# The MLP's first two groups and the fourth of seven products: one more group in seven products, and a weight sum made in SBUF

## The chip, the cores and the metric

The kernel runs on one core of one Trainium2 chip. The metric is the device time of one execution in microseconds (us). A core has five engines with instruction queues of their own: TensorE (PE; its weight loads, PEld, are shown apart), VectorE (DVE), ScalarE (ACT), GpSimd (POOL) and SyncE (SP). They wait for each other through semaphores. SP and POOL issue the transfers of this kernel (DMA); the names SPq and POOLq stand for their queues. An engine works through its instructions in the order in which the program lists them, so an instruction that waits holds up everything behind it.

## The reference

One layer of a hybrid encoder on 512 tokens of width 1024, in float32: an input projection, forgetting attention and a gated linear recurrence side by side, cross-attention to 256 memory tokens, and an MLP.

```
h = h + concat(fox_out, rec) @ w_out
h = h + memory_cross_attention(rmsnorm(h), mem_n, w_xq, w_xkv, w_xo)
u = rmsnorm(h, norm_ff_g) @ w1          # w1: 1024 x 4096
h = h + square(relu(u)) @ w2            # w2: 4096 x 1024
return rmsnorm(h, final_norm_g)
```

This case is about the last three lines.

## The kernel before

**Float32 in three products.** TensorE multiplies in a format of fewer bits (fp32r). So each float32 operand is split into a high part and a low part, and a product is made as hi·hi + hi·lo + lo·hi. A weight block arrives raw from DRAM (`wr…`, issued by SP); ScalarE copies it to its high part (`wh…`, line L181 in `split_of`) and VectorE subtracts that from the raw data for the low part (`wl…`, L185). Both parts have four buffers, so a split can start when the product four places earlier has ended. `unit()` keeps splits up to four units ahead of the products and loads up to eight units ahead (`LOADS`).

**Groups.** The MLP's 4096 hidden columns are worked off in 8 groups of 512. For a group, the *up* set computes u = x2 · W1 for its 512 columns, ScalarE applies relu and square, and the *down* set adds the square times the group's rows of W2 to the residual `acc`. The order is up 0, up 1, down 0, up 2, down 1, and so on to up 7, then down 6 and 7 together.

**Seven products.** An up or a down set may be made like a Strassen-Winograd product: weights and data are each cut into 2 x 2 blocks, and seven products of sums of blocks take the place of eight products of blocks. Before, up sets 2 to 7 (`SEVEN`) and all down sets are made so; up sets 0 and 1 are made in full, from "panels" (`next_panel`, `mlp_up`), in four quarters of 24 matmuls of 512 columns. The weight operands of the seven products, by name, with Wrc the block in row r, column c: "1" is W00, "2" is W10, "3" is W11, "5" is W00 + W01, "7" is W01 + W11, "6" is W11 + "5", "4" is W10 + "6". The products are worked off as 1, 5, 6, 2, 7, 3, 4 (`PRODUCTS`).

**Weight sums.** The four sums of a set (`SUMS`) are made in DRAM, long ahead. SP copies the first block from DRAM to a DRAM tile `wsu…` (up) or `wsd…` (down); POOL then issues an accumulating DMA that adds the second block or sum (`Presum.emit`, L444); and SP loads the result into SBUF like any weight block. In the names that follow, `wsd65` is the sum for product 5 of down set 6. `COPIES` says with which weight panel how many of the copies go out. `PACE` sets the POOL accumulates: from a given amount of TensorE work on, one goes out every so many microseconds of TensorE work, and each is given a wait for the matmul at which its time came.

**An up set of seven products** (`mlp_up7`) uses three banks of PSUM. Product 1 goes to bank U. ScalarE copies U to bank V (`uV<-uU`, L1406), and product 2 is added there. Product 5 goes to bank Y, and ScalarE copies it out to `y5` (L1409). Product 6 is added to U, so it stands behind the copy to V. Then ScalarE copies U to bank Y (`uY<-uU`, L1411), where product 3 is added; product 7 is added to U, so it stands behind that copy. VectorE reads U + y5 into SBUF before product 4 is added to U. A product is 24 matmuls of 256 columns.

**The data's sums.** `x_sums` makes the sums of blocks of x2 that products 5, 6, 3 and 7 need: per sum two or three VectorE instructions (`xs_d`), a ScalarE copy to the high part (`xs_hi`) and a VectorE subtraction (`xs_lo`). In the code before it is stepped in group 1. In group 0, after two of its four quarters, the code squares the residual and adds it up (`sj<-acc`, L1666), makes e2 from that on POOL, and scales the residual by e2 (`acc<-acc,e`, L1673).

**What sets the order.** The code is written in one order, and a scheduler of the framework lists the instructions of each engine, by their dependences and priorities; the splits are written with a lower priority (`ahead(PW)`). So the listed order can differ from the code's.

Of the kernel before, what the change touches and what calls it, by code (L numbers as in the profile page):

```python
# [13 lines left out]
ALU = mybir.AluOpType  # L14
# [3 lines left out]
S = 512  # L18
# [4 lines left out]
WT = 256  # L23
# [3 lines left out]
HG = 512  # L27
# [9 lines left out]
FX = (4.4, 4.4, 5.4, 5.4), (3.3, 3.9, 4.5, 5.1)  # L37
X1, X2, X3, X4 = 1.5, 2.0, 1.5, 2.0
NEG = -3.0e38
SEVEN = (2, 3, 4, 5, 6, 7)  # L40
RAWS, HB, LOADS = 6, 4, 8
COPIES = {7: 2, 16: 1, 17: 0, 21: 1, 29: 2}
PACE = (183.0, 4.6), (306.0, 6.0), (385.0, 9.0)


@with_exitstack
def emit(
# [49 lines left out]
    def s4(shape, name, dt=F32):  # L97
        return s4p.tile([P] + shape, dt, tag="s4", name=name)
# [45 lines left out]
    specs = []  # L144
# [16 lines left out]
        for j in range(4):  # L161
            specs.append(panel(w, j * WT))
    NG = DFF // HG
    for g in range(2):
        for j in range(2):
            specs.append(panel(w1, g * HG + j * WT))
    stream = []
    state = {"used": 0, "halves": 0}
    copies, copied = deque(), set()
    UW, UK = WT + FH, KC // 2  # L170
# [7 lines left out]
    def split_of(hi, lo, raw):  # L178
        def split(what="hl"):
            if "h" in what:  # L180
                ac.activation(hi, raw, AF.Copy)  # L181
            if "v" in what:
                ve.tensor_copy(hi, raw)
            if "l" in what:
                ve.tensor_tensor(lo, raw, f(hi), ALU.subtract)  # L185

        return split

    def load_unit(name, spec, ks, parts=1, between=None):
# [12 lines left out]
        for q in range(parts):  # L202
# [208 lines left out]
    hn_hi, hn_lo = act_tile("hn_hi"), act_tile("hn_lo")  # L411
    xTd = drp.tile([4, P, 2, S], F32, name="xTd")

    SUMS = {"5": ("00", "01"), "7": ("01", "11"), "6": ("11", "5"), "4": ("10", "6")}

    def block1(g, rc):
        r, c = int(rc[0]), int(rc[1])
        n0 = g * HG + c * WT
        return w1[r * S : (r + 1) * S, n0 : n0 + WT].rearrange("(k p) n -> p k n", p=P)

    def block2(g, rc):
        r, c = int(rc[0]), int(rc[1])
        k0 = g * HG + r * 2 * P
        return w2[k0 : k0 + 2 * P, c * S : (c + 1) * S].rearrange("(k p) n -> p k n", p=P)

    wsum = {}

    def sum_jobs(kind, g):
        block, shape = (block1, [P, UK, WT]) if kind == "u" else (block2, [P, 2, S])
        for name in SUMS:  # L430
            wsum[kind, g, name] = drp.tile(shape, F32, name=f"ws{kind}{g}{name}")

        def first(name):
            dma = nc.sync.dma_start(wsum[kind, g, name], block(g, SUMS[name][0]))
            copied.add((kind, g, name))
            return dma

        def sums():
            for name, (_, b) in SUMS.items():
                while (kind, g, name) not in copied:  # L440
                    copies.popleft()()
                src = wsum[kind, g, b] if b in SUMS else block(g, b)
                more = {"max_dma_last_dim": 2048} if b in SUMS else {}
                yield gp.dma_start(wsum[kind, g, name], src, accum_op=ALU.add, **more)  # L444

        return [lambda name=name: first(name) for name in SUMS], sums()

    class Presum:
        def __init__(self):
            self.jobs, self.spent, self.next, self.at = deque(), 0.0, PACE[0][0], None  # L450

# [23 lines left out]
    presum = Presum()  # L475
    sets = []
    for g in range(DFF // HG):
        sets.append(sum_jobs("d", g))
        if g + 2 in SEVEN:
            sets.append(sum_jobs("u", g + 2))  # L480
    for i in range(0, len(sets), 2):
        for some in zip(*(c for c, _ in sets[i : i + 2])):
            copies.extend(some)
# [168 lines left out]
    for hp in range(2):  # L652
        wt = next_panel()
# [265 lines left out]
    for c in range(NT):  # L919
# [162 lines left out]
    for n in range(len(pairs) + 2):  # L1082
        if n < len(pairs):
            p, tb = pairs[n]
# [97 lines left out]
    _, wo_rest = residual(mx_hi, mx_lo, g_x, x1_hi, x1_lo, "wo", ssq1, (4, 5, 6, 7, 0, 1, 2, 3), 1)  # L1182
# [119 lines left out]
    for i in range(2):  # L1302
        gp.dma_start(gfin[i], final_norm_g[i * S : (i + 1) * S].partition_broadcast(P))
    HS = S // 2
    units, unit_q = {}, deque()
    sqs, comb, hbs = {}, {}, {}
    PRODUCTS = ("1", "5", "6", "2", "7", "3", "4")
    QUAD = {"1": "00", "2": "10", "3": "11"}
    raw_n = [0]

    def raw_tile(name):
        raw_n[0] += 1
        if raw_n[0] % RAWS == 4:
            return t4(f"wr{name}")
        if raw_n[0] % RAWS in (0, 2):
            return wrp.tile([P, D], F32, tag="wr", name=f"wr{name}", padded_shape=[P, UK * UW])
        return s4([D], f"wr{name}")

    load_q = deque()

    def add_unit(key, shape, src):

        name = "".join(map(str, key))
        box = []

        def load():
            raw = raw_tile(name).rearrange("p (k n) -> p k n", k=shape[0])
            nc.sync.dma_start(raw, src())
            box.append(raw)

        def prep():
            while not box:
                load_q.popleft()()
            unit = new_parts(shape, name)
            with ahead(PW):
                split_of(unit[0], unit[1], box[0])()
            units[key] = unit

        unit_q.append((key, prep))
        load_q.append(load)  # L1340

    def up_units(g):
        if g in SEVEN:
            for name in PRODUCTS:
                add_unit(("u", g, name), [UK, WT], lambda name=name: block1(g, QUAD[name]) if name in QUAD else wsum["u", g, name])
            return
        for j in range(2):
            for n in range(2):
                add_unit(("u", g, j, n), [UK, WT], lambda j=j, n=n: block1(g, f"{n}{j}"))

    def down_units(gs):
        for name in PRODUCTS:
            for g in gs:
                add_unit(("d", g, name), [2, S], lambda g=g, name=name: block2(g, QUAD[name]) if name in QUAD else wsum["d", g, name])

    def unit(*key):

        while key not in units:
            unit_q.popleft()[1]()
        got = units[key]  # L1360
        at = order.index(key)
        while unit_q and len(order) - len(unit_q) < at + 4:
            unit_q.popleft()[1]()
        while load_q and len(order) - len(load_q) < at + LOADS:
            load_q.popleft()()
        return got
# [266 lines left out]
        dma_a(tb, o)  # L1633
        scale_b(tb, half, o, r, gfin[half])

    for g in range(NG):
        if g >= 2:
            up_units(g)
        if 1 <= g < NG - 1:
            down_units((g - 1,))  # L1640
    down_units((NG - 2, NG - 1))
    order = [k for k, _ in unit_q]
# [2 lines left out]
    def mlp_up_group(g):  # L1645
        if g in SEVEN:
            yield from mlp_up7(g)
            return
        for j in range(2):
            if g < 2:  # L1650
                wt = next_panel()
                if (g, j) == (1, 1):
                    for _ in range(2):
                        unit_q.popleft()[1]()
            else:
                wt = tuple(list(x) for x in zip(*(unit("u", g, j, n) for n in range(2))))
            yield from mlp_up(g, j, wt)

    ups = mlp_up_group(0)
    next(ups)  # L1660
    to_tok(KC - 2)
    to_tok(KC - 1)
    next(ups)
    ms2 = sm(NT, "ms2")
    for tb in range(NT):
        ac.activation(k4([D], f"sj{tb}"), acc[tb], AF.Square, scale=1.0 / 32.0, accum_out=ms2[:, tb : tb + 1])  # L1666
# [4 lines left out]
    gp.tensor_scalar(eps3, eps3, EPS, 0.0, op0=ALU.mult, op1=ALU.add)  # L1671
    for tb in range(NT):
        ac.activation(acc[tb], acc[tb], AF.Copy, scale=e2[:, tb : tb + 1])  # L1673
    for _ in ups:
        pass
    hidden_sums(0)
    sums = x_sums()
    for g in range(1, NG):
        for n, _ in enumerate(mlp_up_group(g)):
            hidden_ahead((g - 1, PRODUCTS[0]), min(n, HB))  # L1680
            if g == 1:
                next(sums, None)
                next(sums, None)
        hidden_sums(g)
        if g < NG - 1:
            for _ in mlp_down((g - 1,)):
                pass
# [34 lines left out]
```

## Time and profile before

| | |
|---|---|
| median of 3 runs | 756.41 us (756.36 to 757.88) |
| profiled execution | 756.48 us, span 754.5 us |
| TensorE busy | 746.1 us, 99% of the span |
| VectorE, ScalarE, POOL busy | 537.4, 431.1, 190.3 us |
| DMA traffic | 162.85 MB, mean 216 GB/s |
| group 0, up 0 and up 1 in full | 430.06 to 474.50 us |
| down 0 | 474.50 to 493.54 us |
| up 3 | 532.76 to 552.91 us |

The span is the stretch of the profiled execution between its first and last instruction; the execution's own time is a little longer. An engine's busy share is an average over the whole; which engine ends last in a stage is read from windows over that stage and from the waits. A row of the timeline gives start, duration, engine, line, operation, output<-inputs, and in brackets how long the engine was idle before it and who ended that. Instructions of one engine overlap a little, so the time from start to start is what one costs in a row.

### The profile page before, as it was taken

To read this page: it belongs to the slowest core of one execution; us is meant where nothing else is said; L and a number is where in the kernel's file an instruction comes from. 1 tells how busy PE (TensorE), PEld (TensorE's weight loads), DVE (VectorE), ACT (ScalarE), POOL (GpSimd) and SP (SyncE) were. 2 spreads that over 40 slices of the span, in tenths; PEclk is the share of its full clock that TensorE was granted. 3 is DMA by queue.
4 is the path that set the end of the run, shared out by engine and by line. 5 is a ranking of instruction groups with operands and counts; after the bars stand their busy time and mean duration, and the time that the engine had idled before them with its cause. 6 is when DMAs were issued, how large, how long until landed. Compare 5 with 4: busy or idle time off the path is not lost.

```text
span 754.5 us, 12053 instructions
## 1 busy us (share of the span) xinstructions
PE 746.1 (99%) x4501; PEld 648.9 (86%) x4501; DVE 537.4 (71%) x844; ACT 431.1 (57%) x715; POOL 190.3 (25%) x274
## 2 busy tenths in 40 slices
PE   9999999999999999999999999999999999999996
PEld 6889888888888988888888888898989899999985
DVE  5647873677878756745546558978787887879697
ACT  5655555655756532334434396657575757574873
POOL 7207531333342237620121211111000111000014
PEclk9999999999999999999999999999999999999999
DMA  8641987567947899996668879898979797977332
GB/s 251 196 117 57 310 262 226 177 225 252 312 165 222 264 280 290 287 245 128 140 151 182 179 127 312 198 314 229 296 186 298 190 281 205 265 220 248 121 112 112
DMA packets 112444, 162.85 MB, mean 216 GB/s; under 512 B 6482, under 2 KB 73595, under 8 KB 112387
## 3 DMA queue, kind: packets, MB, share of 16 engines
q1 hardware_dynamic: 91186, 123.80, 49.9%
q0 software_dynamic: 20608, 37.25, 27.2%
q10 hardware_dynamic: 592, 1.05, 0.4%
q8 instruction: 35, 0.57, 0.3%
q14 instruction: 23, 0.18, 0.1%
HBM read 157.87 MB, written 62.93 MB: 293 GB/s over the span
## 4 chain that ended last, share of the span: by engine, by line
PE 95%; DVE 1%; ACT 1%; POOL 1%; issue 1%; ACTq 0%; POOLq 0%
PE U L1528 4%; PE U L1527 4%; PE U L1529 4%; PE uU L1402 3%; PE uU L1401 3%; PE uU L1400 3%; PE xq L253 2%; PE wo L253 2%; PE xq L254 2%; PE xw L253 2%; PE xq L255 2%; PE xw L255 2%; PE u L255 2%; PE xw L254 2%; PE wo L255 2%; PE u L254 2%
## 5 line engine op out<-in xcount | busy, mean ns | idle before, releaser
L185 DVE TENSOR_TENSOR wld<-wrd,whd 128x1024 fp32r<-128x1024 f32 x56 | 69.6, 1244 | 17.4 <-ACT whd L181 17.3
L181 ACT ACTIVATE whd<-wrd 128x1024 fp32r<-128x1024 f32 x56 | 59.2, 1057 | 24.6 <-PE uV L1401 8.0
L181 ACT ACTIVATE whu<-wru 128x1024 fp32r<-128x1024 f32 x42 | 44.5, 1059 | 44.9 <-PE uU L1401 18.2
L185 DVE TENSOR_TENSOR wlu<-wru,whu 128x1024 fp32r<-128x1024 f32 x42 | 50.4, 1223 | 14.5 <-ACT whu L181 14.4
L1527 PE MATMUL U<-whd,hb 128*128 128x512 f32 x120 | 46.8, 390 | 0.0
L1528 PE MATMUL U<-wld,hb 128*128 128x512 f32 x120 | 46.8, 390 | 0.0
L1529 PE MATMUL U<-whd,hb 128*128 128x512 f32 x120 | 46.7, 389 | 0.0
L444 POOL DMA_DIRECT2D wsd<-in_w_dram x16 | 16.8, 1050 | 91.5 <-PE U L1529 27.9
L444 POOL DMA_DIRECT2D wsd<-wsd x16 | 14.3, 894 | 98.4 <-PE uU L1402 18.0
L1012 POOL TENSOR_SCALAR bi<-nF,Ft 128x128 f32<-128x128 f32 (+3 forms) x32 | 20.7, 656 | 60.2 <-PE pt L1044 34.7
L444 POOL DMA_DIRECT2D wsu<-in_w_dram x12 | 14.1, 1176 | 58.8 <-PE xq L255 11.4
L1155 ACT ACTIVATE x_hi<-hT,gv 128x512 fp32r<-128x512 f32 x16 | 11.5, 717 | 27.7 <-DVE hT L1154 27.7
L1402 PE MATMUL uU<-x_hi,wlu 128*128 128x256 f32 x96 | 27.2, 283 | 0.0
L1400 PE MATMUL uY<-xs_hi,whu 128*128 128x256 f32 x96 | 27.2, 283 | 0.0
L1401 PE MATMUL uY<-xs_lo,whu 128*128 128x256 f32 x96 | 27.2, 283 | 0.0
L1402 PE MATMUL uY<-xs_hi,wlu 128*128 128x256 f32 x96 | 27.2, 283 | 0.0
L1400 PE MATMUL uU<-xs_hi,whu 128*128 128x256 f32 x96 | 27.2, 283 | 0.0
L1401 PE MATMUL uU<-xs_lo,whu 128*128 128x256 f32 x96 | 27.2, 283 | 0.0
L1402 PE MATMUL uU<-xs_hi,wlu 128*128 128x256 f32 x96 | 27.2, 283 | 0.0
L1401 PE MATMUL uU<-x_lo,whu 128*128 128x256 f32 x96 | 27.2, 283 | 0.0
L1400 PE MATMUL uU<-x_hi,whu 128*128 128x256 f32 x96 | 27.1, 283 | 0.0
L1529 PEld LDWEIGHTS U<-whd,hb 128*128 128x128 f32 x120 | 22.5, 188 | 4.7
(995 smaller groups left out, 2655.2 us busy)
## 6 DMA issues: line engine op xcount, KB each, us to landing
wsd<-in_w_dram SPq DMA_DIRECT2D x32, 512.0 KB, 5.7
wrd<-wsd SPq DMA_DIRECT2D x32, 512.0 KB, 6.3
wsu<-in_w_dram SPq DMA_DIRECT2D x24, 512.0 KB, 7.1
wrd<-in_w_dram SPq DMA_DIRECT2D x24, 512.0 KB, 6.2
wru<-wsu SPq DMA_DIRECT2D x24, 512.0 KB, 6.2
wru<-in_w_dram SPq DMA_DIRECT2D x18, 512.0 KB, 5.8
wsd<-in_w_dram POOLq DMA_DIRECT2D x16, 512.0 KB, 8.0
wsd<-wsd POOLq DMA_DIRECT2D x16, 512.0 KB, 6.8
```

The lines of the kernel that those rows point to most:

```text
L181: ac.activation(hi, raw, AF.Copy)
L185: ve.tensor_tensor(lo, raw, f(hi), ALU.subtract)
L253: te.matmul(ps, wh, hi, start=n_ == 0 and not begun, stop=False)
L254: te.matmul(ps, wh, lo, start=False, stop=False)
L255: at = te.matmul(ps, wl, hi, start=False, stop=k == order[-1])
L444: yield gp.dma_start(wsum[kind, g, name], src, accum_op=ALU.add, **more)
L1400: te.matmul(ps[:, i, :], whi[:, k, ws], xh[:, k, :], start=begin, stop=False, skip_group_check=True)
L1401: te.matmul(ps[:, i, :], whi[:, k, ws], xl[:, k, :], start=False, stop=False, skip_group_check=True)
L1402: at = te.matmul(ps[:, i, :], wlo[:, k, ws], xh[:, k, :], start=False, stop=k == UK - 1, skip_group_check=True)
L1527: te.matmul(ps, hi, whi[:, k, :], start=begin, stop=False, skip_group_check=True)
L1528: te.matmul(ps, hi, wlo[:, k, :], start=False, stop=False, skip_group_check=True)
L1529: at = te.matmul(ps, lo, whi[:, k, :], start=False, stop=k == 1, skip_group_check=True)
```

## The change

Two things are changed in the MLP, with the tables that go with them.

1. Group 1's up set is made of seven products as well. Only group 0 still uses panels. `x_sums` is stepped during group 0's last two quarters, and the squares and the scaling of the residual are written behind group 0's loop. (Their lines are L1676 and L1683 then.)
2. The sum for product 4 is no longer made in DRAM. When product 6's raw tile has been split, POOL adds W10 from DRAM onto the raw tile in SBUF (L1349), and product 4's unit is split from that same tile. This holds for up and down sets, 15 in all. It has no load of its own. Product 6's raw tile is kept in `raws` for it; the rotation of the other raw buffers goes from 6 to 5.

```diff
-SEVEN = (2, 3, 4, 5, 6, 7)
-RAWS, HB, LOADS = 6, 4, 8
-COPIES = {7: 2, 16: 1, 17: 0, 21: 1, 29: 2}
-PACE = (183.0, 4.6), (306.0, 6.0), (385.0, 9.0)
+SEVEN = (1, 2, 3, 4, 5, 6, 7)
+RAWS, HB, LOADS = 5, 4, 8
+COPIES = {7: 2, 16: 1, 17: 0, 21: 1}
+PACE = (183.0, 4.7), (306.0, 11.5)
...
-    SUMS = {"5": ("00", "01"), "7": ("01", "11"), "6": ("11", "5"), "4": ("10", "6")}
+    SUMS = {"5": ("00", "01"), "7": ("01", "11"), "6": ("11", "5")}
...
     for g in range(DFF // HG):
+        if g + 1 in SEVEN:
+            sets.append(sum_jobs("u", g + 1))
         sets.append(sum_jobs("d", g))
-        if g + 2 in SEVEN:
-            sets.append(sum_jobs("u", g + 2))
...
-        if raw_n[0] % RAWS == 4:
+        if raw_n[0] % RAWS == 3:
             return t4(f"wr{name}")
...
         def load():
-            raw = raw_tile(name).rearrange("p (k n) -> p k n", k=shape[0])
-            nc.sync.dma_start(raw, src())
+            if part == "4":
+                box.append(raws.pop((kind, g)))
+                return
+            if part == "6":
+                raw = raws[kind, g] = s4(shape, f"wr{name}")
+            else:
+                raw = raw_tile(name).rearrange("p (k n) -> p k n", k=shape[0])
+            if part in SUMS:
+                src = wsum[kind, g, part]
+            else:
+                src = block(g, QUAD[part])
+            nc.sync.dma_start(raw, src)
             box.append(raw)
 
         def prep():
             while not box:
                 load_q.popleft()()
             unit = new_parts(shape, name)
             with ahead(PW):
                 split_of(unit[0], unit[1], box[0])()
+            if part == "6":
+                gp.dma_start(box[0], block(g, "10"), accum_op=ALU.add)
             units[key] = unit
...
-    for g in range(NG):
-        if g >= 2:
-            up_units(g)
-        if 1 <= g < NG - 1:
+    for g in range(1, NG):
+        up_units(g)
+        if g < NG - 1:
             down_units((g - 1,))
...
     next(ups)
+    sums = x_sums()
+    next(sums)
+    next(sums)
+    for _ in ups:
+        next(sums)
+        next(sums)
     ms2 = sm(NT, "ms2")
...
-    for _ in ups:
-        pass
     hidden_sums(0)
-    sums = x_sums()
     for g in range(1, NG):
         for n, _ in enumerate(mlp_up_group(g)):
             hidden_ahead((g - 1, PRODUCTS[0]), min(n, HB))
             if g == 1:
-                next(sums, None)
                 next(sums, None)
```

How the listed order changes is shown at three places. On ScalarE, from group 0's second quarter on, before (`u001` is the bank of group 0's second quarter, `u010` of its third, `sq00` a hidden tile):

```order
L1666 ACTIVATE sj0_4683,ms2_4682<-acc0_4336 128x1024
L1666 ACTIVATE sj1_4685,ms2_4682<-acc1_4337 128x1024
L1666 ACTIVATE sj2_4687,ms2_4682<-acc2_4338 128x1024
L1666 ACTIVATE sj3_4689,ms2_4682<-acc3_4339 128x1024
L1369 ACTIVATE sq00_4633<-u001_4654 128x512
L1673 ACTIVATE acc0_4336<-acc0_4336,e2_4691 128x1024
L1370 ACTIVATE sq00_4633<-sq00_4633 128x512
L1673 ACTIVATE acc1_4337<-acc1_4337,e2_4691 128x1024
L1673 ACTIVATE acc2_4338<-acc2_4338,e2_4691 128x1024
L1673 ACTIVATE acc3_4339<-acc3_4339,e2_4691 128x1024
L181 ACTIVATE wh36a_4700<-wr36a_4702 128x1024
L1369 ACTIVATE sq01_4738<-u010_4712 128x512
```

After, from the third quarter on, first part (`xs_hi` is a sum of x2):

```order
L1377 ACTIVATE sq01_4705<-u010_4679 128x512
L1676 ACTIVATE sj0_4744,ms2_4743<-acc0_4313 128x1024
L1378 ACTIVATE sq01_4705<-sq01_4705 128x512
L1457 ACTIVATE xs_hi_4659<-xs_d_4661 128x1024
L1676 ACTIVATE sj1_4746,ms2_4743<-acc1_4314 128x1024
L1676 ACTIVATE sj2_4748,ms2_4743<-acc2_4315 128x1024
L1676 ACTIVATE sj3_4750,ms2_4743<-acc3_4316 128x1024
L1377 ACTIVATE sq01_4705<-u011_4712 128x512
```

and directly behind these rows:

```order
L1683 ACTIVATE acc0_4313<-acc0_4313,e2_4752 128x1024
L1378 ACTIVATE sq01_4705<-sq01_4705 128x512
L1683 ACTIVATE acc1_4314<-acc1_4314,e2_4752 128x1024
L1683 ACTIVATE acc2_4315<-acc2_4315,e2_4752 128x1024
L1683 ACTIVATE acc3_4316<-acc3_4316,e2_4752 128x1024
L180 ACTIVATE whu16_4774<-wru16_4772 128x1024
L180 ACTIVATE whu12_4781<-wru12_4779 128x1024
L1414 ACTIVATE uV1_4815<-uU1_4771 128x512
```

The squares and the scalings have moved from around the second quarter's relu to the third's and the fourth's; behind them come the splits of up 1's products 6 and 2 and its copy of bank U to V.

On ScalarE in up set 2, before (`whu24` is the high part for product 4):

```order
L181 ACTIVATE whu27_5173<-wru27_5070 128x1024
L1406 ACTIVATE uV2_5170<-uU2_5138 128x512
L1476 ACTIVATE hb12_5302<-sq11_4898 128x512
L181 ACTIVATE whu23_5205<-wru23_5093 128x1024
L1409 ACTIVATE y52_5203<-uY2_5172 128x512
L181 ACTIVATE whu24_5236<-wru24_5117 128x1024
L1411 ACTIVATE uY2_5172<-uU2_5138 128x512
```

and after:

```order
L180 ACTIVATE whu27_5237<-wru27_5136 128x1024
L1414 ACTIVATE uV2_5234<-uU2_5203 128x512
L180 ACTIVATE whu23_5270<-wru23_5160 128x1024
L1417 ACTIVATE y52_5268<-uY2_5236 128x512
L1484 ACTIVATE hb12_5366<-sq11_4770 128x512
L180 ACTIVATE whu24_5301<-wru26_5090 128x1024
L1419 ACTIVATE uY2_5236<-uU2_5203 128x512
```

The split for product 4 stands in its place as before, ahead of the copy of U to bank Y, and now reads `wru26`, the raw tile of product 6.

On POOL around up sets 4 and 5, after (L443 is an accumulate into DRAM, L1349 one into SBUF; `wru46` is the raw tile of product 6 of up 4):

```order
L443 DMA wsd65_232<-in_w2_dram 256x1x512
L443 DMA wsu77_230<-in_w1_dram 512x1x256
L1349 DMA wru46_5900<-in_w1_dram 128x4x256
L443 DMA wsd67_233<-in_w2_dram 256x1x512
L1349 DMA wrd36_6084<-in_w2_dram 128x2x512
L443 DMA wsu76_231<-wsu75_229 256x512
L443 DMA wsd66_234<-wsd65_232 256x512
L1349 DMA wru56_6305<-in_w1_dram 128x4x256
```

Before, this queue held accumulates into DRAM alone, as here for the sums of sets 4 to 6:

```order
L444 DMA wsu56_223<-wsu55_221 256x512
L444 DMA wsd34_220<-wsd36_219 256x512
L444 DMA wsu54_224<-wsu56_223 256x512
L444 DMA wsd45_225<-in_w2_dram 256x1x512
L444 DMA wsu65_229<-in_w1_dram 512x1x256
```

So the accumulates into SBUF stand between those into DRAM, which wait for their place in TensorE's work.

More of the change, by code (lines that the diff above doesn't have):

```diff
@@ L163, in emit @@
     NG = DFF // HG
-    for g in range(2):
-        for j in range(2):
-            specs.append(panel(w1, g * HG + j * WT))
+    for j in range(2):
+        specs.append(panel(w1, j * WT))
     stream = []
@@ L1304, in emit @@
     HS = S // 2
-    units, unit_q = {}, deque()
+    units, raws, unit_q = {}, {}, deque()
     sqs, comb, hbs = {}, {}, {}
@@ L1319, in emit, with add_unit @@
     load_q = deque()
-    def add_unit(key, shape, src):
+    def add_unit(key, shape):
+        kind, g, part = key[:3]
         name = "".join(map(str, key))
+        block = block1 if kind == "u" else block2
         box = []
         def load():
-            raw = raw_tile(name).rearrange("p (k n) -> p k n", k=shape[0])
-            nc.sync.dma_start(raw, src())
+            if part == "4":
[10 more added lines that the diff above has]
+            nc.sync.dma_start(raw, src)
             box.append(raw)
@@ L1342, in up_units @@
     def up_units(g):
[L1343 to L1349, printed above, removed]
+        for part in PRODUCTS:
+            add_unit(("u", g, part), [UK, WT])
     def down_units(gs):
@@ L1353, in down_units @@
             for g in gs:
-                add_unit(("d", g, name), [2, S], lambda g=g, name=name: block2(g, QUAD[name]) if name in QUAD else wsum["d", g, name])
+                add_unit(("d", g, name), [2, S])
     def unit(*key):
@@ L1649, in mlp_up_group @@
         for j in range(2):
[L1650 to L1656, printed above, removed]
+            wt = next_panel()
+            if j == 1:
+                for _ in range(2):
+                    unit_q.popleft()[1]()
             yield from mlp_up(g, j, wt)
```

## The prediction

> **What bounds the kernel now.** I read the page first: span, busy shares, clock, chain.
>
> ```profile
> span 754.5 us, 12053 instructions
> PE 746.1 (99%) x4501; PEld 648.9 (86%) x4501; DVE 537.4 (71%) x844; ACT 431.1 (57%) x715; POOL 190.3 (25%) x274
> PEclk9999999999999999999999999999999999999999
> PE 95%; DVE 1%; ACT 1%; POOL 1%; issue 1%; ACTq 0%; POOLq 0%
> ```
>
> TensorE is busy for 99% of the span, at a clock that is full in every slice, and it is 95% of the chain that ended last. So a product that goes saves its whole time, and every wait that is put in front of a product costs its whole length. The profiled execution took 756.48 us, its span 754.5: 1.98 lie outside. It stands 0.07 over the median of 756.41, so I add and subtract on the median itself. Within 0.2% of it (1.5 us, 754.9 to 757.9) a measurement cannot tell a change of this kernel from none.
>
> Next, windows over stages of the MLP: start and end, length, then busy time and count of each engine, clock, DMA share, GB/s. They are one quarter of group 0 in full products, the other seven quarters of groups 0 and 1, down set 0, and up set 3.
>
> ```profile
> 430.06:435.51 5.45, 5.45 (x26) 4.46 (x25) 4.95 (x6) 1.67 (x2) 1.17 (x1) 1.00 0.98 209
> 436.30:474.50 38.20, 38.20 (x171) 31.62 (x170) 27.47 (x31) 29.52 (x46) 6.37 (x9) 1.00 0.90 217
> 474.50:493.54 19.04, 19.04 (x85) 15.77 (x84) 18.15 (x25) 12.16 (x17) 3.09 (x3) 1.00 0.96 224
> 532.76:552.91 20.15, 20.15 (x169) 20.14 (x168) 13.87 (x15) 13.37 (x18) 2.21 (x2) 1.00 0.99 292
> ```
>
> In each, busy equals length: no gap anywhere. A full quarter is 38.20 / 7 = 5.457, so a full group is 4 x 5.457 = 21.83. An up set of seven products takes 20.15, or 2.879 a product; a down set's product takes 19.04 / 7 = 2.72. DMA shares of 0.9 to 1.0 slow no product here: busy still equals length.
>
> **Part 1, group 1 as seven products.** It saves 21.83 - 20.15 = **-1.68**, all of it on TensorE.
>
> **Part 2, product 6 of up 1 waits for ScalarE.** The squares of acc (sj) and its scaling by e2 move from group 0's second quarter to behind its third. ScalarE's rows of before (start, duration):
>
> ```profile
> 438.39 1.07 ACT L1666 ACTIVATE sj<-acc 128x1024 f32<-128x1024 f32 x1
> 439.43 1.07 ACT L1666 ACTIVATE sj<-acc 128x1024 f32<-128x1024 f32 x1
> 442.55 0.60 ACT L1369 ACTIVATE sq<-u 128x512 f32<-128x512 f32 x1
> 443.03 1.17 ACT L1673 ACTIVATE acc<-acc,e 128x1024 f32<-128x1024 f32 x1
> 444.07 0.64 ACT L1370 ACTIVATE sq<-sq 128x512 f32<-128x512 f32 x1
> 444.59 3.24 ACT L1673 ACTIVATE acc<-acc,e 128x1024 f32<-128x1024 f32 x3
> 447.71 1.05 ACT L181 ACTIVATE wh36a<-wr36a 128x1024 fp32r<-128x1024 f32 x1
> 448.66 1.06 ACT L181 ACTIVATE wh36b<-wr36b 128x1024 fp32r<-128x1024 f32 x1
> 448.80 1.23 DVE L185 TENSOR_TENSOR wl36a<-wr36a,wh36a 128x1024 fp32r<-128x1024 f32 x1 [6.60 <-ACT wh36a L181]
> ```
>
> Durations overlap, so I go from start to start: sj 1.04, relu 0.48, scaling 1.04 (three 3.12), square 0.52, a split's or a sum's 128x1024 copy 0.95. With the quarter of 5.457, group 0's third quarter ends at 436.30 + 2 x 5.457 = 447.21, and products 1 and 5 of up 1 then run from 452.67 to 458.43. By the changed order ScalarE does from about 447.4: relu 0.48, sj 1.04, square 0.52, xs_hi 0.95, three sj 3.12, relu 0.48, scaling 1.04, square 0.52, three scalings 3.12, the splits of product 6 and of 2 1.90, and the copy of bank U to bank V, 0.58 (row 536.68 below): 13.75. Product 6 writes bank U, so it waits for that copy, to 461.2: **+2.8**. Its bounds: 0 if the scheduler's order leaves the copy early enough, and 3.7 if the four sj and their sum reads don't overlap at all (0.21 each). I take the sum of the starts, since these same instructions stand back to back in the rows. The other moved work, the sums of x2 on VectorE, is free: its idle stretch of 6.60 in group 0 (last row above) takes the five 1.23 us operations, and what cover is gone in group 1 the removed splits of panels return.
>
> **Part 3, the split of product 4 waits for a transfer into SBUF.** Product 6 is raw data split as before; then POOL adds W10 onto the raw tile, and ScalarE splits it again for product 4. Behind that split on ScalarE stands the copy of U to bank Y, for which product 7 waits. Up set 3, from 532.76, shows how much room there is:
>
> ```profile
> 535.02 3.50 DVE L185 TENSOR_TENSOR wlu<-wru,whu 128x1024 fp32r<-128x1024 f32 x3
> 536.68 0.58 ACT L1406 ACTIVATE uV<-uU 128x512 f32<-128x512 f32 x1
> 541.47 1.06 ACT L181 ACTIVATE whu<-wru 128x1024 fp32r<-128x1024 f32 x1 [1.34 <-PE uU L1401]
> 542.44 0.58 ACT L1411 ACTIVATE uY<-uU 128x512 f32<-128x512 f32 x1
> ```
>
> The first of the three subtractions, product 6's, ends at 536.25, 3.49 behind the set's start; the accumulate can go at +3.6. Product 7 begins at +4 x 2.879 = 11.52. In front of it lie the split, 0.97 (541.47 to 542.44), the copy, 0.58, and some 0.1 for the signals. So the transfer must land by 9.87: it may take **6.27**. No transfer of this kind, adding into SBUF, is in the trace. Its neighbours (KB each, us to landing):
>
> ```profile
> wru<-in_w_dram SPq DMA_DIRECT2D x15, 512.0 KB, 5.5
> wsd<-in_w_dram POOLq DMA_DIRECT2D x6, 512.0 KB, 8.2
> wsu<-in_w_dram POOLq DMA_DIRECT2D x2, 512.0 KB, 7.7
> DMA to landing us min/median/max: 5.7/7.8/9.8
> hT<-xTd POOLq DMA_DIRECT2D x4, 512.0 KB, 6.6
> 536.10 1.05 POOL L444 DMA_DIRECT2D wsd<-in_w_dram  x1 [8.50 <-PE uU L1402]
> wsd<-in_w_dram POOLq DMA_DIRECT2D x1, 512.0 KB, 9.1
> ```
>
> The first is the same block, plain, by SP into SBUF; the next three are POOL's accumulates into DRAM from 494 to 690 us; hT is a plain POOL transfer into SBUF; the last two are an accumulate at just the place in a set (+3.3) where the new one goes. Bounds 5.5 and 9.1; I take **7.2**, between hT's 6.6 and the accumulates' median 7.8, because the new one shares the target with the one and the adding with the other. Then it lands at 10.8, the copy is done at 12.45, and product 7 waits 0.93. In up 2, 3, 6 and 7: 4 x 0.93 = **+3.7**.
>
> [...]
>
> In up 4 and up 5 one of POOL's remaining DRAM accumulates stands right in front of the new one: in up 4 that of wsu77, waiting for the last matmul of product 1 (+2.88), in up 5 that of wsd66, waiting for the middle of product 1 (+1.44). What a pair costs, two accumulates issued close together show:
>
> ```profile
> 306.46 0.87 POOL L444 DMA_DIRECT2D wsu<-wsu  x1
> wsu<-wsu POOLq DMA_DIRECT2D x1, 512.0 KB, 8.6
> 308.86 1.05 POOL L444 DMA_DIRECT2D wsd<-in_w_dram  x1 [1.53 <-DVE hT L1154]
> wsd<-in_w_dram POOLq DMA_DIRECT2D x1, 512.0 KB, 9.6
> ```
>
> Issued 2.4 apart, they landed 3.4 apart (315.06 and 318.46). So the second lands 3.4 behind the first. In up 4: 2.88 + 7.2 + 3.4 + 1.65 = 15.13 against 11.52, **+3.6**; in up 5 1.44 + 7.2 + 3.4 + 1.65 = 13.69, **+2.1**. Bounds: 0.9 each if the two go side by side, and 3.6 and 2.1 with one behind the other, which I take since the pair behaved so.
>
> In up 1, delayed by 2.8, the accumulate goes at 461.1 and lands at 468.3. The copy to bank Y stands ahead of the split of 4 in ScalarE's order there, so product 7 goes free; product 4, due at 472.8, waits for its split, a subtraction, two instructions between and the sum of U and y5 on VectorE, some 5.0 us in all (0.97, 1.22, the rest an estimate from the 0.6 to 1.2 us of such rows): **+0.5**, bounds 0 and 2.4.
>
> The down sets cost **0**. The bank copies there are not behind the split of 4 within reach:
>
> ```profile
> 551.21 1.23 DVE L185 TENSOR_TENSOR wld<-wrd,whd 128x1024 fp32r<-128x1024 f32 x1 [0.28 <-ACT whd L181]
> ```
>
> This subtraction, down 2's product 6, ends 0.47 ahead of its set (552.91). The accumulate goes at -0.4, and product 4's split is due 3 products on, at 3 x 2.72 = 8.2: up to 8.5 it hides.
>
> **Part 4, what goes.** 11 copies within DRAM, 11 DRAM accumulates and 8 loads fewer, 15 accumulates more, and 72 narrower matmuls for wider ones. Nothing waited for the loads removed (busy equals length above), so their removal gives 0; one raw buffer less and the new pace of the sums also cost 0, as loads run eight units ahead.
>
> **Sum:** -1.68 + 2.8 + 3.7 + 3.6 + 2.1 + 0.5 = +11.0, and 756.4 + 11.0 = 767.4, say **767.5**. Each us of landing above 6.3 is worth about 7 us, since seven up sets pay it.
>
> **Rivals.**
> B, the transfer hides. It lands in 6.2 or less, as SP's 5.5 speaks for and the DRAM accumulates speak against. What is left is part 1 and part 2 (+1.1: 757.5), and at a landing of 6.2 up to 3.8 of the pairs: 757.5 to 761.3. It decides at 6.27.
> C, the transfer is longer, 8.3 or more, as the row at the same place in a set (9.1) speaks for: four sets 4 x 2.0 or more, the pairs 4.7 and 3.2, up 1 1.6, and the down sets begin to wait: 775 to 785.
> D, the other side. ScalarE catches up in up 1: the scaling of acc is needed only by down 0's sums, so it may stand behind the copy to bank V; without those 4.16, 13.75 becomes 9.59, ready at 457.0 before 458.43, and part 2 is 0. It decides at 11.0 of work ahead of the copy. With a landing within 6.27, 754.7 is left. The changed order speaks against it, with the scalings ahead of the copy.
>
> **How the numbers follow.** A, the sum, 0.55; B 0.22; C 0.12; D 0.11. A's own range, with the landing from 6.3 to 8.2, is 761.5 to 774.5. The range for 8 in 10 takes in B from its floor and the near part of C: 757.0 to 776.0. Faster by over 0.2% is D without its half at the edge, and a little of B, 0.10; the lower end of B, up to 757.9, is 0.05 of same; slower 0.85.
>
> **What would show it.** Part 1: a group 1 without panels and up sets of 20.15 plus a stall. Part 2: in group 1 ScalarE's first copy of U to V ends near 461, with TensorE idle ahead of product 6. Part 3: the accumulates into raw tiles land in about 7.2; ScalarE's splits of 4 wait for a DMA; TensorE waits for the copy to bank Y once in each up set, 0.9 in most, more in up 4 and up 5. I am wrong if those landings are near 5.5, if TensorE is without gaps in the up sets, or if it stops in the down sets.

## The result and the profile after

The changed kernel takes 796.32 us (792.48 to 800.2, 6 runs) against 756.41 us: 1.0526 times as long, 95% interval 1.0493 to 1.0559. The forecast was 767.5 with a range up to 776.0. The sign was right; the size was out by a factor of 3.6.

The page of the profiled execution (797.72 us): span, busy shares, chain, and the medians of POOL's new accumulates into SBUF for down and up sets.

```profile
span 796.0 us, 12170 instructions
PE 758.0 (95%) x4573; PEld 663.1 (83%) x4573; DVE 541.0 (68%) x849; ACT 434.6 (55%) x721; POOL 202.5 (25%) x278
PE 67%; issue 17%; DMA 7%; ACT 3%; DVE 2%; POOL 2%; POOLq 0%; SPq 0%; ACTq 0%
wrd<-in_w_dram POOLq DMA_DIRECT2D x8, 512.0 KB, 7.1
wru<-in_w_dram POOLq DMA_DIRECT2D x7, 512.0 KB, 9.0
```

TensorE was busy for 99% of the span and is now for 95%, and 67% of the chain instead of 95%. The windows over up 1, down 0 and up 2 to 7 (length, busy time and count by engine, clock, DMA share, GB/s) show where:

```profile
453.08:482.26 29.18, 22.83 (x169) 22.62 (x168) 21.48 (x24) 24.69 (x35) 4.28 (x5) 0.88 0.56 141
482.26:501.33 19.07, 19.07 (x87) 15.77 (x85) 17.81 (x25) 12.40 (x17) 3.51 (x3) 1.00 0.96 234
501.33:525.79 24.46, 21.65 (x170) 21.45 (x168) 14.72 (x16) 13.36 (x18) 3.42 (x4) 0.93 0.77 201
544.86:569.56 24.70, 21.89 (x169) 21.69 (x168) 14.55 (x16) 13.35 (x18) 3.67 (x4) 0.93 0.76 201
588.63:616.65 28.02, 22.65 (x169) 22.44 (x168) 14.55 (x16) 13.35 (x18) 3.74 (x4) 0.88 0.68 180
635.72:664.17 28.45, 22.87 (x169) 22.66 (x168) 14.56 (x16) 13.35 (x18) 3.47 (x4) 0.88 0.70 175
683.24:709.79 26.55, 21.89 (x170) 21.69 (x168) 14.55 (x16) 13.35 (x18) 2.42 (x3) 0.94 0.68 183
728.86:750.69 21.83, 20.40 (x170) 20.20 (x168) 13.35 (x14) 13.34 (x18) 1.29 (x1) 1.00 0.61 172
```

Down sets are as before. Every up set is longer than 20.15 us, in two ways. Length less busy time is waiting: 6.35, 2.81, 2.81, 5.37, 5.58, 4.66 and 1.43, together 29.0. Busy time above 20.15 is the same 168 matmuls running slower: 2.68, 1.50, 1.74, 2.50, 2.72, 1.74 and 0.25, together 13.1. In up 1 to 6 the granted clock is down to 0.88 to 0.94. In up 7 it is full, so its 0.25 has another cause. With the 1.68 gained, 29.0 + 13.1 - 1.7 = 40.4 of the 41.2 by which the two profiled executions differ.

Whom TensorE waits for (us in total, times, longest):

```profile
PE uU L1408 <- ACT uY L1419: 22.7, 6, 5.6
PE uU L1408 <- ACT uV L1414: 6.4, 1, 6.4
```

The first is product 7 behind the copy of U to bank Y in up 2 to 7, the second product 6 of up 1 behind the copy of U to bank V. Up 2 in the timeline, one piece each of POOL, ScalarE and TensorE:

```profile
505.27 1.31 POOL L1349 DMA_DIRECT2D wru<-in_w_dram  x1 [9.23 <-DVE wlu L184]
...
514.22 1.06 ACT L180 ACTIVATE whu<-wru 128x1024 fp32r<-128x1024 f32 x1 [4.99 <-DMA wru<-in_w_dram]
515.18 0.58 ACT L1419 ACTIVATE uY<-uU 128x512 f32<-128x512 f32 x1
...
515.81 0.58 PE L1408 MATMUL uU<-xs_hi,whu 128*128 128x256 f32 x1 [2.81 <-ACT uY L1419]
```

The accumulate goes at +3.94 and lands 8.86 later; the split of 4 waits for it 4.99 us, the copy stands behind the split, TensorE behind the copy. The first matmul behind the wait takes 0.58 us. The next ones start every 0.21 us until 518.54, then every 0.12 as ahead of the wait. Windows over the stretches of up 1 and up 2 in which the granted clock was 0.50:

```profile
464.05:470.88 6.83, 5.54 (x26) 5.54 (x27) 5.79 (x5) 4.59 (x6) 2.29 (x2) 0.50 0.50 102
515.25:518.66 3.41, 2.85 (x13) 2.85 (x14) 2.45 (x2) 3.23 (x6) 0.00 (x0) 0.50 0.82 167
```

In up 1 to 6 the clock was halved from near the end of the wait on: for 3.4 us in up 2, 3 and 6, for 6.8 us in up 1, 4 and 5.

### The profile page after: what moved, and what is told of

Its sections match the earlier page's. It is cut to its first block, busy times and chain, and to the rows that moved or that the text cites. A ratio compares the mean times of both kernels' runs of the same rounds, so it can differ in the third digit from the quotient of the medians.

```text
span 796.0 us, 12170 instructions
## 1 busy us (share of the span) xinstructions
PE 758.0 (95%) x4573; PEld 663.1 (83%) x4573; DVE 541.0 (68%) x849; ACT 434.6 (55%) x721; POOL 202.5 (25%) x278
## 4 chain that ended last, share of the span: by engine, by line
PE 67%; issue 17%; DMA 7%; ACT 3%; DVE 2%; POOL 2%; POOLq 0%; SPq 0%; ACTq 0%
DMA wru<-in_w_dram 6%; PE uU L1408 2%; PE xq L252 2%; PE wo L252 2%; PE xq L253 2%; PE xq L254 2%; PE xw L252 2%; PE xw L253 2%; PE wo L254 2%; PE wo L253 2%; PE xw L254 2%; PE uU L1409 2%; PE uU L1410 2%; PE U L1535 2%; PE U L1536 2%
## 5 line engine op out<-in xcount | busy, mean ns | idle before, releaser
L184 DVE TENSOR_TENSOR wlu<-wru,whu 128x1024 fp32r<-128x1024 f32 x49 | 58.8, 1219 | 52.7 <-ACT whu L180 52.6
L180 ACT ACTIVATE whu<-wru 128x1024 fp32r<-128x1024 f32 x49 | 51.5, 1054 | 76.9 <-DMA wru<-in_w_dram 43.4
L1408 PE MATMUL uU<-xs_hi,whu 128*128 128x256 f32 x112 | 37.8, 338 | 29.0 <-ACT uY L1419 22.7
L1408 PEld LDWEIGHTS uU<-xs_hi,whu 128*128 128x128 f32 x112 | 26.8, 240 | 30.4 <-ACT uY L1419 23.9
L443 POOL DMA_DIRECT2D wsd<-in_w_dram x16 | 16.8, 1053 | 107.4 <-PE uU L1410 33.0
L1409 PE MATMUL uU<-xs_lo,whu 128*128 128x256 f32 x112 | 36.8, 329 | 0.0
L1410 PE MATMUL uU<-xs_hi,wlu 128*128 128x256 f32 x112 | 36.7, 327 | 0.0
L443 POOL DMA_DIRECT2D wsu<-in_w_dram x14 | 17.1, 1219 | 64.8 <-PE uY L1410 16.2
L1408 PE MATMUL uY<-xs_hi,whu 128*128 128x256 f32 x112 | 31.8, 284 | 0.0
L1409 PE MATMUL uY<-xs_lo,whu 128*128 128x256 f32 x112 | 31.8, 284 | 0.0
L1349 POOL DMA_DIRECT2D wrd<-in_w_dram x8 | 10.1, 1262 | 69.1 <-DVE wld L184 69.1
L1409 PEld LDWEIGHTS uU<-xs_lo,whu 128*128 128x128 f32 x112 | 26.8, 240 | 0.0
```

The source lines that it names most:

```text
L1408: te.matmul(ps[:, i, :], whi[:, k, ws], xh[:, k, :], start=begin, stop=False, skip_group_check=True)
L1409: te.matmul(ps[:, i, :], whi[:, k, ws], xl[:, k, :], start=False, stop=False, skip_group_check=True)
L1410: at = te.matmul(ps[:, i, :], wlo[:, k, ws], xh[:, k, :], start=False, stop=k == UK - 1, skip_group_check=True)
```

## The experiments

Theory: the chain just shown makes the waits of up 2 to 7, ScalarE's order that of up 1, and each wait costs clock behind it. The main rival: group 1 as seven products, with the sums it needs sooner, costs by itself.

**Each part alone.** First group 1 stays in seven products, and the sum for product 4 goes back to DRAM. Its load, the sixth raw buffer, `COPIES` and `PACE` go back with it; of the edit only the two main places are shown.

```diff
-    SUMS = {"5": ("00", "01"), "7": ("01", "11"), "6": ("11", "5")}
+    SUMS = {"5": ("00", "01"), "7": ("01", "11"), "6": ("11", "5"), "4": ("10", "6")}
...
-            if part == "6":
-                gp.dma_start(box[0], block(g, "10"), accum_op=ALU.add)
```

> Group 1 in seven products stays, the sum for product 4 is made in DRAM and loaded, as before the change. Theory (the transfer into SBUF makes product 7 wait in up 2 to 7, and each wait also costs TensorE its clock): up 2 to 7 are 20.15 us again, up 1 keeps its wait for the copy of U to V (29.2 us), so 756.4 - 1.7 + 9.0 = about 764 us. Rival (group 1 as seven products, with the sums of x2 and the DRAM sums it needs sooner, is what costs): most of the 40 us stays, 785 us or more.

763.01 us (762.42 to 763.59); the kernel before took 756.61 beside it. Windows over up 1 and up 2:

```profile
452.93:481.89 28.96, 23.01 (x170) 22.80 (x169) 22.21 (x23) 25.10 (x35) 5.06 (x6) 0.88 0.69 168
500.95:521.11 20.16, 20.16 (x170) 20.15 (x169) 14.37 (x16) 13.49 (x18) 1.76 (x2) 1.00 1.06 318
```

TensorE's one wait of the MLP is left, of product 6 of up 1 for the copy to bank V:

```profile
PE uU L1400 <- ACT uV L1406: 5.9, 1, 5.9
```

Up 2 to 7 are 20.15 or 20.16 us again.

Then the other part alone: up 1 in full, with its panels and its order as before, and the sum for product 4 in SBUF.

```diff
-SEVEN = (1, 2, 3, 4, 5, 6, 7)
+SEVEN = (2, 3, 4, 5, 6, 7)
```

> Up 1 in full as before; only the sum for product 4 is made in SBUF. Theory: up 2 to 7 lose what they lose in the changed kernel (4.3, 4.6, 7.9, 8.3, 6.4 and 1.7 = 33 us, somewhat more or less as the DRAM accumulates fall in front of them), so 784 to 795 us. Rival (group 1 costs): 756 to 760 us.

789.04 us (787.89 to 790.18), beside the same 756.61. The two parts add up: 6.4 + 32.4 = 38.8 of 39.9. Some 32 us are the sum in SBUF, and group 1 in seven products, with the order that came with it, costs 6 us where it should gain 1.7.

**Up 1.** The squares and the scaling of the residual are put back into group 0's second quarter; the rest as changed.

```diff
     next(ups)
+    ms2 = sm(NT, "ms2")
...
+    for tb in range(NT):
+        ac.activation(acc[tb], acc[tb], AF.Copy, scale=e2[:, tb : tb + 1])
     sums = x_sums()
...
-    ms2 = sm(NT, "ms2")
...
-    for tb in range(NT):
-        ac.activation(acc[tb], acc[tb], AF.Copy, scale=e2[:, tb : tb + 1])
     hidden_sums(0)
```

> The squares and the scaling of the residual stand in group 0's second quarter again; the rest as changed. Theory (ScalarE's queue made product 6 of up 1 wait): that wait of 6.4 us is gone with its clock loss of 2.7; but the split of 4 now stands ahead of the copy to bank Y in up 1 too, for a wait like that of up 2 (2.8 and 1.5): 797 - 9.0 + 4.3 = about 792 us. Rival (the sums of x2 come late from VectorE, and ScalarE waits for them): up 1 still loses 6 us or more ahead of product 6, 796 us.

790.68 us (790.66 to 790.71). The copy to bank V is no longer waited for. But up 1 takes 26.7 us, with two waits at product 7, for the fourth sum of x2 (TensorE's timeline):

```profile
466.98 0.58 PE L1408 MATMUL uU<-xs_hi,whu 128*128 128x256 f32 x1 [2.48 <-ACT xs_hi L1457]
468.76 0.58 PE L1409 MATMUL uU<-xs_lo,whu 128*128 128x256 f32 x1 [1.21 <-DVE xs_lo L1461]
```

So both readings had a part: ScalarE's order made the first wait, and behind it the sums of x2 were late, as the rival said, though for product 7 and not 6. In the changed kernel that lateness can be read, too (ScalarE and VectorE in group 0):

```profile
444.33 2.01 ACT L180 ACTIVATE whu<-wru 128x1024 fp32r<-128x1024 f32 x2 [5.48 <-DMA wru<-in_w_dram]
...
449.96 0.58 ACT L1377 ACTIVATE sq<-u 128x512 f32<-128x512 f32 x1
...
453.21 1.06 ACT L1457 ACTIVATE xs_hi<-xs_d 128x1024 fp32r<-128x1024 f32 x1 [1.11 <-DVE xs_d L1454]
...
464.72 0.57 ACT L1414 ACTIVATE uV<-uU 128x512 f32<-128x512 f32 x1
...
445.42 1.23 DVE L184 TENSOR_TENSOR wlu<-wru,whu 128x1024 fp32r<-128x1024 f32 x1 [4.15 <-ACT whu L180]
446.56 1.22 DVE L1454 TENSOR_TENSOR xs_d<-xs_d,x_lo 128x1024 f32<-128x1024 f32 x1
```

ScalarE stands 5.48 us for up 1's first weight block, VectorE 4.15 for ScalarE with a piece of the sum behind that wait, and so the third sum's copy starts at 453.21. The copy to bank V follows at 464.72. The raw buffer that the change gave up is not the reason: with the sum in DRAM and six buffers again, the same split waited 5.05 us, until 443.77.

The next version reorders all of this, with the sum for product 4 in DRAM and its tables as before: the squares in group 0's second quarter, all four sums of x2 begun in group 0, and the scaling tied behind up 1's copy to bank Y (`state["uY"]`). Of the edit the lines on the sums and the scaling are shown.

```diff
     sums = x_sums()
-    next(sums)
-    next(sums)
+    for _ in range(4):
+        next(sums)
     for _ in ups:
         next(sums)
         next(sums)
...
-            if g == 1:
-                next(sums, None)
+            if g == 1 and n == 3:
+                for tb in range(NT):
+                    scaled = ac.activation(acc[tb], acc[tb], AF.Copy, scale=e2[:, tb : tb + 1])
+                    tc.add_manual_dep(scaled.ins, state["uY"].ins.name, sync, reason="later")
```

> Group 1 in seven products, the sum for product 4 in DRAM as before, the squares of the residual in group 0's second quarter, all four sums of x2 begun in group 0, and the scaling of the residual behind up 1's copy of U to bank Y. Theory: no engine is late for up 1 any more, and what is left of the change is its gain: 756.4 - 1.7 = 754.7 us, up 1 at 20.2 us; at most 1.5 us more if the fourth sum is late for product 7. Rival (group 1 as seven products can't be fed in time, whatever the order): up 1 at 23 us or more, 758 us or more.

754.79 us (754.19 to 756.46, 11 runs) against 756.36: 0.9979, interval 0.997 to 0.9988. Up 1 and up 7:

```profile
453.17:473.32 20.15, 20.15 (x169) 20.15 (x168) 17.52 (x20) 18.40 (x25) 3.02 (x3) 1.00 0.92 213
688.49:708.64 20.15, 20.15 (x169) 20.15 (x168) 13.26 (x14) 13.45 (x18) 1.78 (x2) 1.00 0.85 227
```

Group 1 can be fed, and its gain of 0.2% is the one forecast: 1.57 against 1.68. This version is the only one here that is faster than the kernel before. The squares now stand on ScalarE from 438.83 on, where it stood idle, and the split of the first block follows at 444.94 without a wait. The squares alone were not enough, as the run before shows; which of the other two moves is needed was not tried.

**The order on ScalarE in an up set.** In the changed kernel the copy of U to bank Y is tied ahead of the split of 4.

```diff
+            if part == "4" and kind == "u":
+                tc.add_manual_dep(state["split"].ins, state["uY"].ins.name, sync, reason="copy first")
```

> On ScalarE the copy of U to bank Y is forced ahead of the split of product 4 in each up set; the transfer is as late as before. Theory (the order on ScalarE turns a late landing into a wait of product 7): product 7 runs on, and product 4, 5.8 us later, has the split in time, all but 1 us in the sets where a DRAM accumulate stands in front. Up 2 to 7 at 20.2 to 21.2, up 1 still 29: 764 to 768 us. Rival (the transfer only moves the wait, from product 7 to product 4): up sets at 23 us or more, 780 us or more.

782.24 us (781.98 to 782.51): in the rival's range, well above the 768 forecast. Up 2, 3 and 7 are nearly free (21.1, 20.8, 20.2), but up 4, 5 and 6 take 26.2, 25.7 and 24.8. Up 4, TensorE's wait in its timeline, and VectorE ahead of it:

```profile
603.18 0.35 PE L1411 MATMUL uU<-x_hi,whu 128*128 128x256 f32 x1 [4.38 <-DVE sq L1426]
...
598.69 1.23 DVE L184 TENSOR_TENSOR wlu<-wru,whu 128x1024 fp32r<-128x1024 f32 x1 [8.56 <-PE uY L1412]
599.84 1.22 DVE L184 TENSOR_TENSOR wld<-wrd,whd 128x1024 fp32r<-128x1024 f32 x1
601.75 0.69 DVE L1491 TENSOR_TENSOR hb<-s,hb 128x512 fp32r<-128x512 f32 x1 [0.69 <-ACT hb L1487]
602.36 0.68 DVE L1426 TENSOR_TENSOR sq<-uU,y 128x512 f32<-128x512 f32 x1
```

VectorE stood 8.56 us at the subtraction of 4 (the releaser that its row names had long been done; the accumulate landed at 597.52 and ScalarE's split of it began at 597.60). The sum U + y5, for which product 4 waits, is listed behind that, behind a subtraction of the next down set and behind a piece of the hidden data. The landing was taken out of one queue and met again in the next: the rival was right for the sets with a late landing.

**What makes the landing late.** The DRAM accumulates are paced at 6.0 in place of 11.5, so that none is left on POOL from up 4 on.

```diff
-PACE = (183.0, 4.7), (306.0, 11.5)
+PACE = (183.0, 4.7), (306.0, 6.0)
```

> The changed kernel, with the DRAM accumulates paced at 6.0 in place of 11.5, so that from up 4 on none stands on POOL beside the accumulates into SBUF. Theory (a neighbour lengthens the transfer, from some 8.5 us alone to some 11.5): up 4, 5 and 6 land in 8 to 9 us and take 22 to 24.5 us in place of 28.0, 28.5 and 26.6, some 12 us less in all; up 2 or 3, which now have the neighbours, up to 4 more: 784 to 790 us. Rival (the length is the transfer's own): up 4 to 6 as long as in the changed kernel, 796 us.

792.61 us (789.79 to 795.43). Windows of up 2, 4 and 5:

```profile
500.58:530.24 29.66, 22.88 (x170) 22.67 (x168) 14.77 (x16) 13.35 (x18) 4.94 (x5) 0.83 0.82 202
...
597.55:619.94 22.39, 20.40 (x170) 20.20 (x168) 14.44 (x16) 13.47 (x18) 1.49 (x2) 1.00 0.69 194
639.01:661.37 22.36, 20.41 (x170) 20.21 (x169) 14.44 (x16) 13.47 (x18) 1.49 (x2) 1.00 0.65 194
```

The accumulates of up 2 and of up 4 (KB, us to landing):

```profile
wru<-in_w_dram POOLq DMA_DIRECT2D x1, 512.0 KB, 12.8
...
wru<-in_w_dram POOLq DMA_DIRECT2D x1, 512.0 KB, 8.0
```

Where the neighbours went, the loss went: up 4 and 5 from 28.0 and 28.5 to 22.4, with landings of 8.0 and 8.2; up 2 and 3, now with a neighbour directly in front, from 24.5 and 24.7 to 29.7 and 29.2. The total missed the forecast of 784 to 790 and is within the changed kernel's own spread, as the losses mostly moved. Up 6 and 7, alone on POOL, still landed in 9.0 and 9.5, and up 7 went from 21.8 to 24.7 with that.

Next the rows' length: in the up sets POOL adds a contiguous block (the sum for product 6, rows of 4 KB) in place of W10 (rows of 1 KB). Product 4's weight is then made without W10.

```diff
-                gp.dma_start(box[0], block(g, "10"), accum_op=ALU.add)
+                gp.dma_start(box[0], wsum[kind, g, "6"] if kind == "u" else block(g, "10"), accum_op=ALU.add)
```

> The changed kernel, but in the up sets POOL adds the contiguous sum for product 6 from DRAM onto the raw tile in place of W10, so the rows read are 4 KB long and not 1 KB (product 4 then has another weight). Theory (the transfer of many short rows is slow): the up accumulates that stand alone land in 6 to 7.5 us, like those of the down sets with their rows of 2 KB, and up 2, 3 and 7 wait for at most 1 us: 780 to 786 us. Rival (an accumulate into SBUF takes 8 to 9 us whatever its rows): 796 us.

781.28 us (779.04 to 783.51). Windows of up 2, up 4 and up 7:

```profile
500.56:520.87 20.31, 20.31 (x170) 20.21 (x169) 14.37 (x16) 13.57 (x18) 3.04 (x3) 1.00 0.85 244
...
580.14:609.48 29.34, 21.93 (x170) 21.73 (x168) 14.56 (x16) 13.35 (x18) 3.37 (x4) 0.88 0.64 170
716.33:736.48 20.15, 20.15 (x170) 20.15 (x168) 13.26 (x14) 13.45 (x18) 0.90 (x1) 1.00 0.62 186
```

The accumulates of up 2 and of up 4:

```profile
wru<-wsu POOLq DMA_DIRECT2D x1, 512.0 KB, 6.1
...
wru<-wsu POOLq DMA_DIRECT2D x1, 512.0 KB, 13.4
```

With none in front, the same 512 KB land in 6.0 to 6.9 instead of 8.2 to 9.0, and up 2, 3 and 7 lose 0.2, 1.0 and nothing. With a DRAM accumulate 0.6 us in front (up 4) it is 13.4 all the same; with one 1.9 and 3.3 us in front (up 5 and 6) it is 8.9 and 9.4.

The source changed here together with the rows: one contiguous DRAM tile in place of a piece of W1. The transfers of before, into DRAM, show that this could matter by itself, as these two have rows of 2 KB each:

```profile
wsd<-in_w_dram POOLq DMA_DIRECT2D x16, 512.0 KB, 8.0
wsd<-wsd POOLq DMA_DIRECT2D x16, 512.0 KB, 6.8
```

For the rows speak the changed kernel's down sets: with 2 KB rows of W2 and none in front, their accumulates into SBUF landed in 5.7 (down 0 and down 5) and 7.4 (the first of the last two sets). So the rows are the likelier cause, but the two were not separated.

**The start.** The sum for product 4 gets a raw tile of its own: SP loads the sum for product 6 there once more, and POOL adds W10 without waiting for product 6's split. There are six raw buffers again, and up 1 is ordered as in the fast version.

```diff
-            if part in SUMS:
-                src = wsum[kind, g, part]
+            if part in SUMS or part == "4":
+                src = wsum[kind, g, "6" if part == "4" else part]
...
             nc.sync.dma_start(raw, src)
+            if part == "4":
+                gp.dma_start(raw, block(g, "10"), accum_op=ALU.add)
```

> The sum for product 4 is made in SBUF, but in a raw tile of its own: SP loads the sum for product 6 there a second time, ahead like any other weight block, and POOL adds W10 at once, without waiting for product 6's split. Up 1 is ordered as in the last version of e5 (squares in group 0, scaling behind the copy to bank Y). Theory (what costs is that the transfer can start only at the split of 6, 3.6 to 4 us into the set, and not that it adds into SBUF): the accumulates take 8 to 12 us as before, but land before the split of 4 is due; no up set is longer than 20.2 us, except one or two with a DRAM accumulate beside, by up to 2 us: 754.7 to 757 us. Rival (accumulates into SBUF are too slow for this pace wherever they start, or hold up POOL's DRAM sums): 760 us or more.

763.94 us (761.69 to 767.39): a miss, in the rival's range. Up 1 and 7 are free, but in up 3 the accumulate starts only 0.8 us into the set, behind its load, and lands 12.5 later. Its window, and the transfer:

```profile
533.19:556.97 23.78, 20.41 (x169) 20.20 (x168) 14.38 (x16) 13.39 (x18) 3.54 (x4) 1.00 0.80 225
```

```profile
wru<-in_w_dram POOLq DMA_DIRECT2D x1, 512.0 KB, 12.5
```

An earlier start bought 3 us in up 3, and the longer landing took all of that back. Up 4, 5 and 6 landed in 12.5, 12.2 and 10.6. In all four sets the accumulate ahead on POOL had landed at least 2.5 us before this one was issued, so a neighbour in front is not the only thing that lengthens a landing. What else does isn't settled; SP's additional load in each set was not varied.

**The clock.** The changed kernel with 24 matmuls more, into a bank that nobody reads, between products 2 and 7 of up 2 to 6.

```diff
+                if 2 <= g <= 6:
+                    spare = tr(f"spare{g}")
+                    for k in range(4 * UK + 2 * UK):
+                        te.matmul(spare[:, :HS], whi[:, k % UK, 0:P], xh[:, k % UK, :], start=True, stop=True, skip_group_check=True)
```

> The changed kernel with 24 matmuls more (2.9 us of work into a bank that nobody reads) between products 2 and 7 of up 2 to 6, where TensorE waits. Theory (part of each loss, 1.5 to 2.7 us, is TensorE's clock, which is halved for some us after a wait): the added work fills the wait, the clock stays, and up 2 and 3 take 23.0 us in place of 24.5 and 24.7, up 4 to 6 some 1 us less each; all in all 788 to 791 us, so more work is faster by some 6 us. Rival (the slow matmuls behind a wait have another cause): 796 us or more, up to 796 + 5 x 2.9 = 810 us.

795.1 us (794.85 to 795.36). Windows of up 2, 5 and 6:

```profile
501.47:524.50 23.03, 23.03 (x193) 23.03 (x192) 14.79 (x16) 13.26 (x18) 3.43 (x4) 1.00 0.83 213
...
638.09:663.07 24.98, 23.28 (x193) 23.07 (x192) 14.38 (x16) 13.14 (x18) 3.38 (x4) 1.00 0.78 198
682.14:707.01 24.87, 23.29 (x193) 23.08 (x192) 14.38 (x16) 13.14 (x18) 2.34 (x3) 1.00 0.71 189
```

Up 2 has 2.88 us more work and is 1.43 faster, exactly 20.15 + 2.88, at full clock. Up 5 and 6 are 3.5 and 1.7 faster; their busy time is 20.15 + 2.88 + 0.25, where it had a surplus of 2.7 and 1.7. So the slow matmuls come from the wait ahead of them. The total fell by 1.2 us only, which is within the spread of the changed kernel, and not by the 6 expected: the accumulates of up 3 and 4 took 11.3 and 14.2 us this time instead of 9.0 and 11.4, and these sets 25.5 and 30.9.

## Why the prediction was wrong

**Part 1 (-1.68) was right:** 1.57 in the version in which nothing waits, with up 1 at 20.15.

**Part 2 (+2.8) named the right wait, mis-sized:** 6.35 of waiting and 2.68 of clock. The step that failed is "free" for the sums of x2 on VectorE, and a ScalarE queue that starts at 447.4 with nothing behindhand. Both engines had lost 4 to 5 us to up 1's first weight block by then (rows above). ScalarE came to the third quarter's relu only at 449.96, and then waited another 1.1 us for the third sum; its copy to bank V ended at 465.29 instead of 461.2. That this block's late landing is the whole cause is read from the trace and was not tried.

**Part 3's mechanism was right, its landing and its price per us were not.** The formula holds: for up 2, 3.94 + 8.86 + 1.65 = 14.45, and product 7 began at 14.48. What was put in was wrong: 7.2 for a landing that was 8.2 to 9.0 with no DRAM accumulate in front and 10.9 to 11.6 with one. The reason given, "because the new one shares the target with the one and the adding with the other", left out the length of the rows. The trace of before has POOL's accumulates of the same 1 KB rows, over the whole run:

```profile
wsu<-in_w_dram POOLq DMA_DIRECT2D x12, 512.0 KB, 8.3
```

The run with 4 KB rows, from another source, landed in 6.0 to 6.9. At 9.0 the rival C was due, which had 0.12; without a clock term it too came to 785 at most. The neighbour's price was too low as well: the second of a pair landed 5.0 us behind the first in up 4 and up 5, not 3.4. Up 6 had a neighbour too (10.9) and was forecast without: it waited 4.66 instead of 0.93. In up 1 product 4's +0.5 did not come: its set shows only the one wait. The shortest landing of POOL's accumulates before, 5.7, holds for 494 to 690 us; over the whole trace it is 5.3.

**The missing term is the clock.** "Every wait that is put in front of a product costs its whole length" lacked the clock behind it: 13.1 us (0.25 of them, in up 7, at full clock), and in up 2, 2.81 of waiting cost 4.31. The kernel before has no gap in this part, so its trace could not show it. The trace of the changed kernel shows it: behind the wait of 2.81 us in up 2 the matmuls start every 0.21 us in place of 0.12, with the granted clock at 0.50 for 3.4 us; behind the 1.43 of up 7 it stays at 1.00.

**Part 4 and the down sets at 0 were right:** 19.07 each, with landings of 5.7 to 9.1 there. Part 4 counts 8 loads fewer; with the four panels of up 1 it is 12, at no cost either.

With the measured waits and clock in their places, the sum is -1.7 + 9.0 (up 1) + 33.1 (up 2 to 7) = 40.4; with the waits alone it would be 27.3, 784 us. So of the 29 us that the forecast missed, the longer waits are 16 and the clock 13.

## What to carry to other kernels

Where TensorE is busy all the time, price a new wait with the clock that it can lose: in these runs 0.25 us more for waits of up to 2.4 us, and 1.5 to 3.0 us more from 3.75 us on, with no fixed share of the length (1.8 for the longest, 7.4). Take the duration of a transfer not in the trace from one with the same row length and kind of source as well as the same queue (here 8.3 for POOL's accumulates of 1 KB rows before, against 8.2 to 9.0 after), and ask what stands on that queue in front of it (10.9 to 11.6 with one accumulate ahead). And a late operand moved ahead in one in-order queue is met again in the next (VectorE stood 8.56 us at it in up 4, with the copy tied ahead): follow it through every engine to the product, before and after.

## What was unexpected

- The same wait length did not always cost the clock. The up sets of all runs that have one wait fall into three kinds. Sixteen waits of up to 2.4 us cost 0.22 to 0.26 us more than their length, at full clock. Of eleven from 2.66 to 3.37 us, nine cost 1.5 to 1.75 more, with the clock at half for 3.4 us; the other two, among them the 3.37 of up 3 with a tile of its own (busy 20.41, clock 1.00), cost 0.25. All twenty-one from 3.75 us on cost 1.5 to 3.0 more. What decides between the two outcomes from 2.66 to 3.37 us was not shown.
- An accumulate of 512 KB onto SBUF by POOL took from 5.7 us, in down 0 of the changed kernel, to 14.2, in up 4 with the spare matmuls. The rows and a neighbour in front account for part of that: 1 KB rows with none in front mostly took 8.0 to 9.5, but 6.5 in up 1 with the squares early, 11.3 in up 3 with the spare matmuls, and up to 12.5 with a tile of its own. The changed kernel's time varies by 1% (792.5 to 800.2), the kernel before by 0.3%; that the landings make the difference is likely, but only one execution of each was traced.
